# Rotary embedding in three operations ahead of the head norms, queries' norm and transposes beside the key product, first loads on two queues

## The chip, the cores and the metric

The kernel runs on one core of one Trainium2 chip. The metric is the device time of one execution in microseconds (us), as the median of several executions. Engines are called PE (TensorE matmul, with PEld for its weight loads), DVE (VectorE), ACT (ScalarE), POOL (GpSimd) and SP (SyncE, which here only issues DMAs). Each engine works through its own instructions in order; what a program leaves to the scheduler is only the order in which they stand there.

## The reference

The reference is a network in two parts over a sequence of 256 tokens with 1024 features, all in float32. The change touches only the first part's projections and the latent attention ("b") that follows them:

```python
def apply_rope(x, positions):               # r = 32
    ang = positions[..., None] * inv_freq
    cos = jnp.cos(ang)[:, :, None, :]; sin = jnp.sin(ang)[:, :, None, :]
    x1, x2 = xf[..., : r // 2], xf[..., r // 2:]
    out = jnp.concatenate([x1 * cos - x2 * sin, x2 * cos + x1 * sin], axis=-1)
...
xn = rms_norm(h, norm_mix_g)
proj = jnp.einsum('bsd,de->bse', xn, w_in)
qa, ka, va, c_q, c_kv, k_rope = jnp.split(proj, cuts, axis=-1)
qa = rms_norm(qa.reshape(b, s, 8, 64), qnorm_a_g)
ka = rms_norm(ka.reshape(b, s, 8, 64), knorm_a_g)
...
qb = jnp.einsum('bsr,re->bse', rms_norm(c_q, cq_norm_g), w_uq).reshape(b, s, 8, 96)
kv = jnp.einsum('bsr,re->bse', rms_norm(c_kv, ckv_norm_g), w_ukv)
k_nope, vb = kv[..., :64], kv[..., 64:]
kb = jnp.concatenate([k_nope, broadcast(k_rope)], axis=-1)
qb = rms_norm(qb, qnorm_b_g); kb = rms_norm(kb, knorm_b_g)
qb = jnp.concatenate([qb[..., :64], apply_rope(qb[..., 64:], positions)], axis=-1)
kb = jnp.concatenate([kb[..., :64], apply_rope(kb[..., 64:], positions)], axis=-1)
out_b = causal_block_attention(qb, kb, vb)
```

Behind it come the output product, a feed-forward network, and the second part (two layers with attention, 32 experts and a gated embedding). The rotation turns pairs of a head's features with the same angle, so it leaves the head's sum of squares as it is; a head's norm factor is the same before and after it.

## The kernel before

Tokens lie on the partitions in two tiles t of 128. Weights stream from HBM through an arena of 21 buffers in panels that SP issues in program order (L299). A float32 product is made of three matmuls: `split` (L528 to 538) takes a weight block and writes a rounded copy hi and the remainder lo into one of five `s` buffers. The copy is made by ACT (L536), every sixth by POOL (L534); the subtraction by DVE (L537), every fifth by POOL (L537). `mm3` (L540 to 543) then issues x_hi·hi (L541), x_hi·lo (L542) and x_lo·hi (L543), per k block of 128 features and per t: six matmuls for a k block. `steps_of` splits two blocks ahead.

PE and SP execute in the order of the code. ACT, DVE and POOL get their order from a scheduler that goes by its own estimates. What follows a product (copies out of PSUM, squares for the norms) is put into the list `late` and issued by `flush` after the first two splits of the next product.

The order of the first part: transposes of x (`xt_feats`, L501, evicted by ACT L518 and DVE L519), product cq in two halves (the other transposes of x go on beside the first), the tables of the rotation (L1278 to 1307), ckv, qa, uq (two halves of 384 columns, evicted by `uq_done`, L1373), ukv (evicted by `ukv_done`, L1403), ka (`kproj`, L1411), va (`vproj`, L1440), transposes of the normed queries and keys of attention b (`heads_T`, L1454 and L1455: PE L730, ACT L731), then the attention stream (L1491), into which the rest of va is woven. `Rstd` (L481 to 496) squares x on ACT (L488), four operations, and makes the row factor r. `head_ss` squares on ACT (L603) and sums on DVE (L604). `rsqrt` (L456 to 479) is a chain of DVE operations; one call, 32 values wide, serves queries and keys (L1418 to 1420). After it POOL multiplies the queries by their factor (L1424, two instructions), DVE rotates queries and keys (`rope`, L752 to 762: six operations for the queries' t and six for the keys' t), DVE and POOL norm the keys (L1428, L1430). All this is written between the first k block of ka and the rest of it.

At the start, SP issues the identity, two tiles of x, the first weight panel, two more tiles of x and further panels; ACT issues `small`, the table of gains (L382 to 404).

## Time and profile before

| | |
|---|---|
| median of 3 runs | 880.39 us (879.73 to 885.22) |
| the profiled execution | 883.1 us, span in the trace 881.3 us |
| mean granted PE clock | 0.971 |
| PE busy | 829.3 us (94%) |
| DVE busy | 512.2 us (58%) |
| ACT busy | 453.0 us (51%) |
| POOL busy | 225.0 us (26%) |
| DMA | 200.05 MB, mean 227 GB/s |

The median is the kernel's time. The span is what the trace covers; 1.8 us of the profiled execution lie around it. Busy shares are means over stages with different limits, so what matters is which wait of PE ends last in a stage. [...] Matmul rows that follow one another closely are pipelined, so the distance from start to start is what one costs, not its own length.

### The profile page before, as it was taken

To read this page: it belongs to the slowest core of one execution; us is meant where nothing else is said; L and a number is where in the kernel's file an instruction comes from. 1 tells how busy PE (TensorE), PEld (TensorE's weight loads), DVE (VectorE), ACT (ScalarE), POOL (GpSimd) and SP (SyncE) were. 2 spreads that over 40 slices of the span, in tenths; PEclk is the share of its full clock that TensorE was granted. 3 is DMA by queue.
4 is the path that set the end of the run, shared out by engine and by line. 5 is a ranking of instruction groups with operands and counts; after the bars stand their busy time and mean duration, and the time that the engine had idled before them with its cause. 6 is when DMAs were issued, how large, how long until landed. Compare 5 with 4: busy or idle time off the path is not lost. (4 is left out here: it accounts for less than half of the span.)

```text
span 881.3 us, 15729 instructions
## 1 busy us (share of the span) xinstructions
PE 829.3 (94%) x5660; PEld 647.4 (73%) x5660; DVE 512.2 (58%) x1479; ACT 453.0 (51%) x1106; POOL 225.0 (26%) x293
## 2 busy tenths in 40 slices
PE   8997999999999999999899999965899899999997
PEld 5995878999999988686667666635587778666656
DVE  5669656755454567678664544321688765543355
ACT  6675875544444456267675133420666774232463
POOL 2225542322222234214453200000122355000011
PEclk9998999999999999999799999995999899999999
DMA  9990429655556542446015699999463515799961
GB/s 307 385 375 31 146 81 399 237 191 171 198 179 188 182 144 96 161 141 237 1 50 197 254 378 406 408 397 379 157 207 129 208 66 193 293 384 406 408 262 49
DMA packets 85137, 200.05 MB, mean 227 GB/s; under 512 B 5776, under 2 KB 27584, under 8 KB 85056
## 3 DMA queue, kind: packets, MB, share of 16 engines
q1 hardware_dynamic: 82704, 195.61, 61.1%
q10 hardware_dynamic: 2352, 3.40, 1.1%
q8 instruction: 46, 0.75, 0.3%
q14 instruction: 35, 0.29, 0.1%
HBM read 197.93 MB, written 1.06 MB: 226 GB/s over the span
## 5 line engine op out<-in xcount | busy, mean ns | idle before, releaser
L537 DVE TENSOR_TENSOR s<-a,s 128x512 fp32r<-128x512 f32 (+3 forms) x281 | 189.5, 685 | 121.7 <-ACT s L536 87.0
L536 ACT CAST s<-a 128x512 fp32r<-128x512 f32 (+3 forms) x294 | 172.6, 600 | 169.8 <-PE pj L543 71.7
L541 PE MATMUL pj<-s,a 128*128 128x512 f32 (+3 forms) x456 | 176.1, 386 | 4.6 <-ACT a L518 3.0
L542 PE MATMUL pj<-s,a 128*128 128x512 f32 (+3 forms) x456 | 170.5, 374 | 5.9 <-DVE s L537 5.8
L543 PE MATMUL pj<-s,a 128*128 128x512 f32 (+3 forms) x456 | 170.4, 374 | 1.3 <-DVE a L519 1.2
L537 POOL TENSOR_TENSOR s<-a,s 128x512 fp32r<-128x512 f32 (+3 forms) x71 | 90.1, 1269 | 304.6 <-ACT s L536 246.6
L541 PEld LDWEIGHTS pj<-s,a 128*128 128x128 f32 x456 | 86.4, 190 | 24.1 <-issue 5.6
L534 POOL TENSOR_SCALAR s<-a 128x512 fp32r<-128x512 f32 (+3 forms) x58 | 40.3, 696 | 242.3 <-PE pj L543 113.9
L542 PEld LDWEIGHTS pj<-s,a 128*128 128x128 f32 x456 | 86.7, 190 | 20.1 <-DVE s L537 7.8
L543 PEld LDWEIGHTS pj<-s,a 128*128 128x128 f32 x456 | 86.6, 190 | 18.2 <-DVE a L519 3.6
L1517 PE MATMUL f<-a,s 128*128 128x256 f32 x256 | 72.6, 284 | 0.0
L1519 PE MATMUL f<-a,s 128*128 128x256 f32 x256 | 72.4, 283 | 0.0
L1518 PE MATMUL f<-a,s 128*128 128x256 f32 x256 | 72.4, 283 | 0.0
L1027 PE MATMUL gu<-a,xe 128*32 128x256 f32 x1024 | 58.7, 380 | 0.7 <-DVE xe L1002 0.7
L1027 PEld LDWEIGHTS gu<-a,xe 128*32 128x32 f32 x1024 | 32.5, 110 | 28.4 <-issue 4.9
L541 PE MATMUL acc<-s,a 128*128 128x512 f32 x128 | 50.1, 391 | 0.0
L542 PE MATMUL acc<-s,a 128*128 128x512 f32 x128 | 49.9, 390 | 0.0
L543 PE MATMUL acc<-s,a 128*128 128x512 f32 x128 | 49.8, 389 | 0.0
L1518 PEld LDWEIGHTS f<-a,s 128*128 128x128 f32 x256 | 49.1, 192 | 0.2
L1517 PEld LDWEIGHTS f<-a,s 128*128 128x128 f32 x256 | 49.1, 192 | 0.2
L1519 PEld LDWEIGHTS f<-a,s 128*128 128x128 f32 x256 | 49.1, 192 | 0.0
L638 POOL TENSOR_SCALAR P<-P,nd 128x128 f32<-128x128 f32 x64 | 30.2, 483 | 58.7 <-DVE nd L633 18.1
(365 smaller groups left out, 1426.1 us busy)
## 6 DMA issues: line engine op xcount, KB each, us to landing
a<-in_w_ff_dram SPq DMA_DIRECT2D x32, 1024.0 KB, 5.5
a<-in_moe_w_gate_dram SPq DMA_DIRECT2D x64, 512.0 KB, 6.8
a<-in_moe_w_up_dram SPq DMA_DIRECT2D x64, 512.0 KB, 7.5
a<-in_moe_w_down_dram SPq DMA_DIRECT2D x32, 1024.0 KB, 8.8
a<-in_a_w_in_dram SPq DMA_DIRECT2D x10, 1024.0 KB, 5.1
a<-in_ple_w_gate_dram SPq DMA_DIRECT2D x8, 1024.0 KB, 15.6
a<-in_w_in_dram SPq DMA_DIRECT2D x6, 1024.0 KB, 14.4
a<-in_w_o_dram SPq DMA_DIRECT2D x4, 1024.0 KB, 13.8
```

The lines of the kernel that those rows point to most:

```text
L534: G.tensor_scalar(hi, wv, 1.0, 0.0, OP.mult, OP.add)
L536: A.copy(hi, wv)
L537: (G if nsplit[0] % 5 == 2 else V).tensor_tensor(lo, wv, hi.bitcast(F32), OP.subtract)
L541: mm(ps, xh, hi, start=st, stop=False)
L542: mm(ps, xh, lo, start=False, stop=False)
L543: mm(ps, xl, hi, start=False, stop=sp)
L638: G.tensor_scalar(p[:, o0:o0 + n], p[:, o0:o0 + n], rc[:, t, i:i + 1], 1.0, OP.mult, OP.mult)
L1027: mm(b[32 * e:32 * e + 32, 0:256], T.xe[:, k, 32 * e:32 * e + 32], w, start=k == 0, stop=k == 7)
L1517: mm(o, hi[:, fs], xt[0][:, k], start=st, stop=False)
L1518: mm(o, hi[:, fs], xt[1][:, k], start=False, stop=False)
L1519: mm(o, lo[:, fs], xt[0][:, k], start=False, stop=sp)
```

## The change

Four things are done. The tiles of x for features 0 to 511 are issued by ACT ahead of `small`, and SP issues the first weight panel in their place. The squares of x and the chain for r are written after the first half of cq instead of ahead of the transposes. The rotation's table holds cos and sin (with the sign in it) for both halves, so a rotation is two multiplications and an addition, in place; the keys' rotation is done for both t at once in `ckv_done`, the queries' in `uq_done(1)`, before the norms. `rsqrt` is called apart for queries and keys, 16 wide; the queries' factor, and POOL's multiplication by it, are issued in `uq_done(1)`. The queries' transposes are woven into ka's k blocks on PE; the keys' stay where they were.

```diff
--- before.py
+++ after.py
@@ -386,10 +386,12 @@
     h = take("h", [2, D])
     W = Stream(arena, weights())
     small = const.tile([128, I["c_small"].shape[1]], F32, name="small")
-    nc.scalar.dma_start(small, I["c_small"])
     for c in range(2):
         for t in range(2):
-            nc.sync.dma_start(h[:, t, c * 512:(c + 1) * 512], I["x"][0, t * 128:(t + 1) * 128, c * 512:(c + 1) * 512])
+            (nc.sync if c else nc.scalar).dma_start(h[:, t, c * 512:(c + 1) * 512],
+                                                    I["x"][0, t * 128:(t + 1) * 128, c * 512:(c + 1) * 512])
+        if not c:
+            nc.scalar.dma_start(small, I["c_small"])
         W.room(NB - 1 - 2 * c)
     posi = const.tile([128, 2], I32, name="posi")
     nc.sync.dma_start(posi, I["positions"].rearrange("o (t p) -> p (o t)", p=128))
@@ -749,17 +751,13 @@
                 v = v.rearrange(f"p ({' '.join(names)}) -> p {' '.join(names)}", **dict(zip(names, shape)))
             return v
 
-    def rope(dst1, dst2, x1, x2, w, t, nh, eng):
-        sh = [128, nh, 16]
-        tb = [rt[:, w, i, t].unsqueeze(1).to_broadcast(sh) for i in range(4)]
-        uvzy = sq2("ru")[:, 0:64 * nh].rearrange("p (a h d) -> p a h d", a=4, h=nh)
-        u, v, z, y = [uvzy[:, i] for i in range(4)]
-        eng.tensor_tensor(u, x1, tb[0], OP.mult)
-        eng.tensor_tensor(v, x2, tb[1], OP.mult)
-        eng.tensor_tensor(z, x2, tb[2], OP.mult)
-        eng.tensor_tensor(y, x1, tb[3], OP.mult)
-        eng.tensor_tensor(dst1, u, v, OP.subtract)
-        eng.tensor_tensor(dst2, z, y, OP.add)
+    def rope(dst, x, tb):
+
+        n = x.shape[1]
+        u, v = sq2("ru")[:, 0:64 * n].rearrange("p (w h a d) -> w p h a d", w=2, a=2, d=16)
+        V.tensor_tensor(u, x, tb[0], OP.mult)
+        V.tensor_tensor(v, x[:, :, ::-1], tb[1], OP.mult)
+        V.tensor_tensor(dst, u, v, OP.add)
 
 
     def load_wr(l):
@@ -1253,13 +1251,7 @@
     st = Stage(STAGE)
     xt = new_xt("xt")
     rs = Rstd("r1")
-    for c in range(2):
-        for t in range(2):
-            rs.add(c, t)
     drain(xt_feats(hsrc, 0, 4, [(xt, "mix", 0)]))
-    r = rs.get()
-    r2 = st(2)
-    V.tensor_tensor(r2, r, r, OP.mult)
 
     ssx = st(8)
     cq = take("cq", [2, 768])
@@ -1274,6 +1266,12 @@
 
     drain(proj(xt, "cq", 384, cq_done(0),
                mid=xt_feats(hsrc, 4, 8, [(xt, "mix", 0)])))
+    for c in range(2):
+        for t in range(2):
+            rs.add(c, t)
+    r = rs.get()
+    r2 = st(2)
+    V.tensor_tensor(r2, r, r, OP.mult)
 
     pf = tiny.tile([128, 2], F32, tag="pf", name="pf")
     V.tensor_copy(pf, posi)
@@ -1296,15 +1294,15 @@
     V.tensor_scalar(kk, kk, -1.0, math.pi / 2, OP.mult, OP.add)
     A.activation(sn, ang, AF.Sin)
     A.activation(cs, kk, AF.Sin)
-    rt = st(2, 4, 2, 16)
+    rt = st(2, 2, 2, 2, 16)
     for w in range(2):
         ro, _n = _SMALL_COLS[("ropeq", "ropek")[w]]
         g1 = small[:, ro:ro + 16].unsqueeze(1).to_broadcast([128, 2, 16])
         g2 = small[:, ro + 16:ro + 32].unsqueeze(1).to_broadcast([128, 2, 16])
-        V.tensor_tensor(rt[:, w, 0], cs, g1, OP.mult)
-        V.tensor_tensor(rt[:, w, 1], sn, g2, OP.mult)
-        V.tensor_tensor(rt[:, w, 2], cs, g2, OP.mult)
-        V.tensor_tensor(rt[:, w, 3], sn, g1, OP.mult)
+        V.tensor_tensor(rt[:, w, 0, :, 0], cs, g1, OP.mult)
+        V.tensor_tensor(rt[:, w, 0, :, 1], cs, g2, OP.mult)
+        V.scalar_tensor_tensor(rt[:, w, 1, :, 0], sn, -1.0, g2, OP.mult, OP.mult)
+        V.tensor_tensor(rt[:, w, 1, :, 1], sn, g1, OP.mult)
 
 
     vps = bank("vps")
@@ -1331,6 +1329,8 @@
             A.activation(junk[:, :256], ps[t][:, 0:256], AF.Square, accum_out=ssx[:, 4 + t:5 + t])
             A.activation(junk[:, 256:288], ps[t][:, 256:288], AF.Square, scale=r[:, t:t + 1],
                          accum_out=sskr[:, t:t + 1])
+        kv = kr.rearrange("p t (a d) -> p t a d", a=2)
+        rope(kv, kv, [rt[:, 1, i] for i in range(2)])
 
     drain(proj(xt, "ckv", 288, ckv_done))
     qk = take("qk", [2, 2, 512])
@@ -1370,6 +1370,12 @@
 
     qbr = take("qbr", [2, 8, 96])
     ssq = st(2, 2, 8)
+    rsb = st(2, 2, 8)
+
+    def rsqrt_b(i):
+        xb = tiny.tile([128, 32], F32, tag="xb", name="xb", bufs=1)[:, 0:16]
+        V.tensor_scalar(xb, ssq[:, i].rearrange("p t h -> p (t h)"), 1.0 / 96, EPS, OP.mult, OP.add)
+        rsqrt(rsb[:, i].rearrange("p t h -> p (t h)"), xb, 16)
 
     def uq_done(c):
         def f(ps):
@@ -1377,6 +1383,13 @@
                 pv_ = ps[t].rearrange("p (h d) -> p h d", d=96)
                 A.activation(qbr[:, t, 4 * c:4 * c + 4], pv_, AF.Copy, scale=rqk[:, t:t + 1])
                 head_ss(ssq[:, 0, t, 4 * c:4 * c + 4], pv_, 4, 96, rqk[:, t:t + 1])
+            if c:
+                for t in range(2):
+                    qv = qbr[:, t, :, 64:96].rearrange("p h (a d) -> p h a d", a=2)
+                    rope(qv, qv, [rt[:, 0, i, t].unsqueeze(1).to_broadcast([128, 8, 2, 16]) for i in range(2)])
+                rsqrt_b(0)
+                for t in range(2):
+                    G.tensor_tensor(qbr[:, t], qbr[:, t], rsb[:, 0, t].unsqueeze(2).to_broadcast([128, 8, 96]), OP.mult)
         return f
 
     for c in range(2):
@@ -1414,27 +1427,21 @@
 
     for t in range(2):
         V.tensor_scalar(ssq[:, 1, t], ssq[:, 1, t], sskr[:, t:t + 1], None, OP.add)
-    xb = tiny.tile([128, 32], F32, tag="xb", name="xb", bufs=1)
-    V.tensor_scalar(xb, ssq.rearrange("p a t h -> p (a t h)"), 1.0 / 96, EPS, OP.mult, OP.add)
-    rsb = st(2, 2, 8)
-    rsqrt(rsb.rearrange("p a t h -> p (a t h)"), xb, 32)
+    rsqrt_b(1)
     kbr = take("kbr", [2, 8, 96])
-    krr = st(2, 32)
     for t in range(2):
-        G.tensor_tensor(qbr[:, t], qbr[:, t], rsb[:, 0, t].unsqueeze(2).to_broadcast([128, 8, 96]), OP.mult)
-        rope(qbr[:, t, :, 64:80], qbr[:, t, :, 80:96], qbr[:, t, :, 64:80], qbr[:, t, :, 80:96], 0, t, 8, V)
-        rope(krr[:, t, 0:16].unsqueeze(1), krr[:, t, 16:32].unsqueeze(1),
-             kr[:, t, 0:16].unsqueeze(1), kr[:, t, 16:32].unsqueeze(1), 1, t, 1, V)
         V.tensor_tensor(kbr[:, t, :, 0:64], kvb[:, t, :, 0:64],
                         rsb[:, 1, t].unsqueeze(2).to_broadcast([128, 8, 64]), OP.mult)
-        G.tensor_tensor(kbr[:, t, :, 64:96], krr[:, t].unsqueeze(1).to_broadcast([128, 8, 32]),
+        G.tensor_tensor(kbr[:, t, :, 64:96], kr[:, t].unsqueeze(1).to_broadcast([128, 8, 32]),
                         rsb[:, 1, t].unsqueeze(2).to_broadcast([128, 8, 32]), OP.mult)
     caus = take("caus", [256])
     V.tensor_scalar(caus, C("ndm"), -1e33, NEG, OP.is_lt, OP.mult)
     dil = take("dil", [8, 256])
     v0 = vd[:, :]
     nc.scalar.dma_start(dil, bass.AP(tensor=v0.tensor, offset=v0.offset, ap=[[1, 128], [384, 8], [1, 256]]))
-    drain(kproj)
+    qTb = take("qTb", [8, S])
+    weave(kproj, heads_T(qTb, lambda t, f: qbr[:, t, f], 8, 96, qsc[:96, 1:2]), 0.7, -1.0)
+    drop("qbr")
 
 
     vproj = proj(xt, "va", 512, qkv_done(2))
@@ -1449,11 +1456,9 @@
             (V if t else G).tensor_tensor(qv, qv, rsa[:, c, t].unsqueeze(2).to_broadcast([128, 8, 64]), OP.mult)
     for _ in range(2):
         next(vproj)
-    qTb = take("qTb", [8, S])
     kTb = take("kTb", [8, S])
-    drain(heads_T(qTb, lambda t, f: qbr[:, t, f], 8, 96, qsc[:96, 1:2]))
     drain(heads_T(kTb, lambda t, f: kbr[:, t, f], 8, 96, gain("kb", 0, 96)))
-    drop("qbr", "kbr")
+    drop("kbr")
     qTa = take("qTa", [4, S])
     kTa = take("kTa", [4, S])
     mixT = new_xt("mixT")
```

POOL, around the key product, before. `s` are the split buffers, a_262 is the panel of ukv, a_282 and a_361 are the two panels of ka, a_399 and a_446 those of va, a_641 the queries, a_877 the keys:

```order
L537 TENSOR_TENSOR s<-a_262,s 128x512
L534 TENSOR_SCALAR s<-a_262 128x512
L534 TENSOR_SCALAR s<-a_361 128x512
L537 TENSOR_TENSOR s<-a_282,s 128x512
L537 TENSOR_TENSOR s<-a_399,s 128x512
L1424 TENSOR_TENSOR a_641<-a_641,stage 128x768 x2
L534 TENSOR_SCALAR s<-a_399 128x512
L1430 TENSOR_TENSOR a_877<-stage 128x8x32 x2
```

And of the change (line numbers are two higher for the same code; a_236 is ukv, a_256 and a_361 are ka, a_399 is va, a_645 the queries, a_906 the keys):

```order
L539 TENSOR_TENSOR s<-a_236,s 128x512
L536 TENSOR_SCALAR s<-a_236 128x512
L1392 TENSOR_TENSOR a_645<-a_645,stage 128x768 x2
L536 TENSOR_SCALAR s<-a_361 128x512
L539 TENSOR_TENSOR s<-a_256,s 128x512
L539 TENSOR_TENSOR s<-a_399,s 128x512
L1435 TENSOR_TENSOR a_906<-stage 128x8x32 x2
L536 TENSOR_SCALAR s<-a_399 128x512
```

The queries' multiplication has moved from behind all of ka's splits to ahead of them: ahead of the copy of ka's block 5 (first panel row a_361) and the subtraction of ka's block 3 (a_282 before, a_256 now).

DVE, from the last subtractions of ukv on, before:

```order
L537 TENSOR_TENSOR s<-a_262,s 128x512 x3
L604 TENSOR_REDUCE stage<-sq 128x4 x2
L537 TENSOR_TENSOR s<-a_282,s 128x512 x2
L604 TENSOR_REDUCE stage<-sq 128x4 x3
L1416 TENSOR_SCALAR stage<-stage 128x8
L604 TENSOR_REDUCE stage<-sq 128x4
L1416 TENSOR_SCALAR stage<-stage 128x8
L537 TENSOR_TENSOR s<-a_282,s 128x512
```

And of the change, from the same place:

```order
L539 TENSOR_TENSOR s<-a_236,s 128x512 x3
L606 TENSOR_REDUCE stage<-sq 128x4
L758 TENSOR_TENSOR ru<-a_645,stage 128x256
L759 TENSOR_TENSOR ru<-a_645,stage 128x256
L606 TENSOR_REDUCE stage<-sq 128x4
L760 TENSOR_TENSOR a_645<-ru 128x8x32
L758 TENSOR_TENSOR ru<-a_645,stage 128x256
L759 TENSOR_TENSOR ru<-a_645,stage 128x256
L1377 TENSOR_SCALAR xb<-stage 128x16
L539 TENSOR_TENSOR s<-a_256,s 128x512
L760 TENSOR_TENSOR a_645<-ru 128x8x32
L470 TENSOR_SCALAR rs<-xb 128x16
```

The queries' rotation and the start of their factor now stand between ukv's subtractions and ka's. Between the subtractions of ka's block 1 and block 2 stand then the rest of that chain (nine operations), four sums and the two additions that were L1416 and are L1429.

ACT, at the start, before (a_109 is the second panel of cq, a_99 is x, a_142 its transpose):

```order
L536 CAST s<-a_109 128x384
L488 ACTIVATE junk,ss<-a_99 128x512 x4
L518 ACTIVATE a_142<-tps,small 128x256 x2
L536 CAST s<-a_109 128x384
L518 ACTIVATE a_142<-tps,small 128x256
L536 CAST s<-a_109 128x384
```

And of the change:

```order
L538 CAST s<-a_109 128x384
L490 ACTIVATE junk,ss<-a_99 128x512
L520 ACTIVATE a_142<-tps,small 128x256
L490 ACTIVATE junk,ss<-a_99 128x512 x2
L520 ACTIVATE a_142<-tps,small 128x256 x2
L490 ACTIVATE junk,ss<-a_99 128x512
L538 CAST s<-a_109 128x384
L520 ACTIVATE a_142<-tps,small 128x256
```

The four squares have not left this place: the scheduler puts them between the same evictions, now one after one square instead of after four.

## Rows read from the trace of the kernel before

**Rows 1.** Waits of PE, 0 to 140 us; us in total, times, longest.
```profile
PE pj L542 <- DVE s L537: 5.4, 2, 5.0
PE pj L541 <- ACT a L518: 1.3, 1, 1.3
...
PE pj L543 <- DVE a L519: 0.8, 2, 0.6
```

**Rows 2.** Timeline of PE: start, length, instruction, xcount, idle before and releaser.
```profile
69.65 0.39 PE L541 MATMUL pj<-s,a 128*128 128x512 f32 x1
70.41 0.50 PE L542 MATMUL pj<-s,a 128*128 128x512 f32 x1 [0.37 <-DVE s L537]
...
79.88 0.39 PE L541 MATMUL pj<-s,a 128*128 128x512 f32 x1
85.28 0.80 PE L542 MATMUL pj<-s,a 128*128 128x512 f32 x1 [5.01 <-DVE s L537]
...
89.87 3.66 PE L730 MATMUL htp<-ident_r,a 128*96 128x128 f32 x32
```

**Rows 3.** Windows: busy time of each engine in each stretch.
```profile
core 0: us, PE busy (x) PEld busy (x) DVE busy (x) ACT busy (x) POOL busy (x), PEclk, DMA share, GB/s
4.00:5.00 1.00, 1.00 (x6) 0.47 (x5) 0.00 (x0) 0.00 (x0) 0.00 (x0) 1.00 0.56 142
...
80.00:85.30 5.30, 0.29 (x3) 0.02 (x1) 5.30 (x26) 1.71 (x3) 2.10 (x3) 0.76 0.00 0
85.30:88.00 2.70, 2.70 (x6) 2.13 (x7) 2.70 (x5) 0.18 (x1) 2.30 (x2) 0.50 0.00 0
```

**Rows 4.** Timeline of DVE, 61 to 94 us.
```profile
62.22 0.69 DVE L537 TENSOR_TENSOR s<-a,s 128x512 fp32r<-128x512 f32 x1 [2.35 <-POOL s L534]
62.83 1.01 DVE L604 TENSOR_REDUCE stage<-sq 128x4 f32<-128x384 f32 x2
...
68.51 0.67 DVE L1416 TENSOR_SCALAR stage<-stage 128x8 f32<-128x8 f32 x1
...
69.67 0.69 DVE L537 TENSOR_TENSOR s<-a,s 128x512 fp32r<-128x512 f32 x1
70.27 1.27 DVE L1418 TENSOR_SCALAR xb<-stage 128x32 f32<-128x32 f32 x1
...
81.14 0.28 DVE L759 TENSOR_TENSOR ru<-a,stage 128x128 f32<-128x128 f32 x1
81.35 0.28 DVE L760 TENSOR_TENSOR ru<-a,stage 128x128 f32<-128x128 f32 x1
...
84.54 0.68 DVE L537 TENSOR_TENSOR s<-a,s 128x512 fp32r<-128x512 f32 x1
...
91.37 0.18 DVE L465 TENSOR_TENSOR rs<-rs 128x32 f32<-128x32 f32 x1
...
92.72 0.19 DVE L479 SCALAR_TENSOR_TENSOR stage<-rs 128x32 f32<-128x32 f32 x1
```

**Rows 5.** Timeline of POOL, 55 to 94 us.
```profile
68.53 0.62 POOL L534 TENSOR_SCALAR s<-a 128x512 fp32r<-128x512 f32 x1 [6.35 <-DMA a<-vd]
70.13 1.37 POOL L537 TENSOR_TENSOR s<-a,s 128x512 fp32r<-128x512 f32 x1 [0.97 <-POOL s L534]
...
76.60 3.86 POOL L1424 TENSOR_TENSOR a<-a,stage 128x768 f32<-128x768 f32 x2 [0.81 <-DVE stage L479]
```

**Rows 6.** Timeline of all engines, 0 to 20 us.
```profile
1.18 0.89 SPq L392 DMA_DIRECT2D a<-in_x_dram  x2
...
2.12 0.43 SPq L299 DMA_DIRECT2D a<-in_w_in_dram  x1
...
8.66 0.44 PE L541 MATMUL pj<-s,a 128*128 128x384 f32 x1 [1.25 <-ACT a L518]
...
11.75 0.63 ACT L488 ACTIVATE junk<-a 128x512 f32<-128x512 f32 x1
...
17.49 0.44 PE L543 MATMUL pj<-s,a 128*128 128x384 f32 x1 [0.64 <-DVE a L519]
```

## The prediction

> **What bounds the kernel now.** The page says that PE is busy 94% of the span, so a change elsewhere pays only where PE waits. I therefore read the waits of PE first, for 0 to 140 us, the stretch in which the diff moves anything; behind the attention the order of all engines is the same but for some rows of DVE. [rows 1] Few waits are left there: 5.4 us for DVE's lo of a split (two waits, one of them 5.0), 1.3 for ACT's copy of a transpose and 0.8 for DVE's. The first is in the key and value products, the others are at the head.
>
> I then looked at PE's timeline around the long wait. [rows 2] From 70.41 to 79.88 stand 41 matmuls, so one costs 9.47 / 41 = 0.23 us. In ka's block 2 the L541 of 69.65 is followed by an L542 at 70.41 instead of 69.88: 0.5 late. In va's block 1 the L541 of 79.88 is followed by an L542 at 85.28 instead of 80.11: 5.2 late. From there 11 matmuls take 85.28 to 89.87 = 4.59 us; at 0.23 they would take 2.5, so another 2.1 go. [...] So this stage loses 0.5 + 5.2 + 2.1 = 7.8 us, and that is what the change can win here.
>
> DVE's timeline says what it is late with: [rows 4] va's subtraction starts at 84.54, right after 24 rope operations on the same engine, which are done from 79.05 to 84.54. Nothing is slow about the subtraction itself, it is queued.
>
> **What the change removes and adds.** The rope operations leave that place, so the 5.2 and the 2.1 go, unless something takes their place. I follow the new DVE queue from the end of ukv's subtractions, 62.83 (the start of what follows the last one of 62.22). [rows 4]
> - Two sums, 1.01 for both, started 0.95 apart from what follows.
> - Six rope operations of 128x256. The trace has 128x128, whose starts lie 0.20 apart (81.14, 81.35), and 128x512 in the subtraction, 0.61 (62.22 to 62.83). Between them 128x256 is 0.20 + 0.41 / 3 = 0.34; six make 2.0. The bounds are 0.20 (1.2) and 0.61 (3.7).
> - Three small operations at about 0.1 (0.3) and ka's first two subtractions, 0.61 each (1.2). That is 67.3; ka's block 0 and 1 need theirs at 67.1 and 68.5 (69.65 less 11 and less 5 matmuls), and block 0's stands one place earlier, at about 66.2. Both are in time.
> - The rest of the queries' chain: before, eight dependent operations from 91.37 to 92.72 with the last one's 0.19 make 1.54; one more is 0.17. So the queries' factor is ready at T0 = 69.0.
>
> Now POOL starts the queries' multiplication: 3.86 us for two [rows 5], to 72.95. Behind it in POOL's queue stand two pieces of the key product, as the order shows: the copy of ka's block 5 (0.62, before at 68.53), then the subtraction of ka's block 3 (1.37, before at 70.13). That subtraction now ends at 69.0 + 0.1 + 3.86 + 0.62 + 1.3 = 74.9, and PE's L542 of block 3 is due at 69.88 + 6 x 0.23 = 71.3. So PE waits 3.6 us there even if nothing else is late. This is the first price of the change.
>
> The second is on DVE. It has four sums and two additions of 128x8 ahead of the subtraction of ka's block 2. Such an addition took 0.67 at 68.51 with POOL's copy beside it (68.53, 0.62), and the 1.27 of L1418 at 70.27 end at 71.54 with POOL's subtraction (70.13 to 71.50) [rows 4, 5]: DVE stood still until POOL's instruction ended. Beside 1.93-us instructions of POOL the same gives: sums to 70.1, first addition to 71.0, second to 72.95, the subtraction after POOL's copy at 73.6, done at 74.2. So the L542 of ka's block 2 starts at 74.25 instead of 69.88, 4.4 late, and block 3's at 75.6 finds its lo ready. I take 4.4; the lower bound is the 3.6 above, the upper one comes with the rope operations at 0.61: T0 is 1.7 later, so 6.1.
>
> [...]
>
> A wait of 4.4 us is nearly as long as the 5.0 that halved the clock. I take the same clock loss, 2.1, with bounds 0 (the clock holds) and 3.1 (it stays low half as long again). So the stage loses 6.5 after and 7.8 before: 1.3 us won.
>
> **The other parts.** The queries' 16 transposes move from after the value blocks into ka. All 32 take 3.66 us on PE [rows 2] and each costs the same anywhere, so 0; the queries are ready at 72.95, and the first transposes stand behind ka's block 3, which ends after 76. If that cover went, PE would wait for POOL there instead of at block 3, no more. The keys' rotation is now three DVE operations of 128x64 at under 0.20 each [rows 4] beside the qa product, whose subtractions have 1 to 2 us in hand: 0; without that cover 0.5. The rotation's table has eight operations as before: 0. Queries' and keys' `rsqrt` apart add nine small operations, about 1.5 us of DVE, which hold back the later subtractions of ka; these follow PE's own delay: 0, and 1.5 without that cover.
>
> At the head, SP spent 0.89 us on two tiles of x before the first panel (issued at 2.12) [rows 6]; now ACT issues these tiles and the panel goes 0.9 earlier. The first matmul, at 8.66, waited 1.25 for ACT, which had begun when the panel landed. Not all of the 0.9 arrives, since the tiles and the panel share the transfers; in 4 to 5 us the DMA share was 0.56 [rows 3], so there was a gap of 0.4 us to fill. The squares (0.63 each [rows 6]) hold up the copies out of PSUM: the waits of the second set, up to the 0.64 at 17.49. In the new order one copy stands after one square, but all four are still ahead of a copy of cq's block 6, so most of that wait moves there. I take 1.0 for the head; the bounds are 0 and the 2.1 of all its waits [rows 1].
>
> [...]
>
> **Sum.** 1.3 + 1.0 = 2.3. The profiled execution took 883.1, of which 1.8 lie around the span of 881.3; it becomes 880.8. It is 2.7 above the median, which becomes 880.4 - 2.3 = 878.1.
>
> **The rivals.**
> - The clock holds through the new wait (0.2). It is shorter than the one before, and on both sides of it PE works without gaps. Against it: 5.0 us sufficed before, and the new one is only 0.6 shorter. The 2.1 are won too: 876.0.
> - Slower than before (0.15): the new wait is longer than the old. Place: the subtraction of ka's block 2 and the queue ahead of it. If the rope operations cost 0.61 each, the wait is 6.1, and with 3.1 for the clock the stage loses 9.2 instead of 7.8; with a head that wins nothing, 881.8. It decides when that subtraction ends later than 69.88 + 5.7 = 75.6 (5.7 + 2.1 is the 7.8 of before), with the head's 1.0 later than 76.6. For it: the operand is in strided pieces of 16, which no row of before has in this size. Against it: 128x128 in the same strides was at 0.20.
> - The key product does not wait (0.07). POOL's two splits would have to be ready in time, which needs the queries' factor before about 65.5; by the queue above it is not there before 68. The whole 7.8 and the head's 1.0 are won: 871.6.
> - The two queues do nothing (0.03): the transfers share the same engines and the first panel lands when it did. Then 1.0 less is won: 879.1.
>
> **How the numbers follow.** The forecast has 0.55, with a range of its own from 876.5 (wait 3.6, head 1.8) to 879.7 (wait 5.4, head 0.4). The rivals have 0.2, 0.15, 0.07 and 0.03. The range from 874.0 to 882.0 takes in the forecast, the held clock with its own 2 us, the slower case and the two queues; it leaves out the case without a wait and the tails of the others. A measurement can tell about 1%, 8.8 us. To win that much, the whole 7.8 and over 1.0 at the head would be needed: 0.04. To lose it, the new wait would have to be some 11 us longer than forecast, which no row bears out: 0.02. Within 1%: 0.94.
>
> **What would show it.** Right: in the trace after, no long wait at va's block 1; an L542 of ka's block 2 (or 3) some 4 us late, released by DVE or by POOL's subtraction; POOL's two 128x768 instructions at about 69 to 73, with DVE's additions beside them stretched to over 1 us; a granted clock of 0.50 after it; the first panel's matmul at about 8.0. Wrong: rope operations at over 0.4 us; POOL's multiplication starting before 67 or after 71; a wait at va's block 0 or 1 as before, now behind the keys' norm; or waits at the head that are all still there.

## The result, and the profile after

The changed kernel takes 876.09 us in the median of 6 runs (872.97 to 876.67), the kernel before 881.51 in 6 runs beside it (879.73 to 885.22). The ratio is 0.9929 with a 95% interval of 0.9903 to 0.9955. The profiled execution took 875.73, its span is 873.9; PE is busy 824.7 us (94%), the mean granted clock, the share of PE's full clock that the chip granted, is 0.979 (0.971 before). So the change gains 5.4 us, 0.6%; the forecast was 2.3 us (878.1), with a range of 874.0 to 882.0. A later comparison, with 5 runs of the changed kernel and 17 of the one before, gave 875.84 and 880.13: 4.3 us.

Line numbers of the changed kernel are two higher in the helpers: L543, L544, L545 are the three matmuls of `mm3`, L539 the subtraction, L536 POOL's copy. The waits of PE in its trace, 0 to 140 us (us in total, times, longest), answer to [rows 1]:

```profile
PE pj L544 <- DVE s L539: 3.8, 3, 2.5
PE warm L378 <- DVE xc L1739: 1.1, 1, 1.1
PE pj L543 <- ACT a L520: 0.8, 1, 0.8
PE tps L503 <- DMA a<-in_x_dram: 0.8, 1, 0.8
PE ops L656 <- ACT PT L650: 0.2, 1, 0.2
```

The 5.0 us in the value product are gone. In their place stands one wait of 2.5 for DVE's subtraction (the other 1.3 us of that first line are two waits at the head, 0.2 and 1.1), and the waits for the head's copies, 1.3 and 0.8 before, have become one of 0.8. PE's timeline (start, length, instruction, idle before and its releaser), around the new wait, against [rows 2]:

```profile
69.19 0.39 PE L543 MATMUL pj<-s,a 128*128 128x512 f32 x1
72.10 0.53 PE L544 MATMUL pj<-s,a 128*128 128x512 f32 x1 [2.52 <-DVE s L539]
...
76.08 0.40 PE L545 MATMUL pj<-s,a 128*128 128x512 f32 x1
```

It is in ka's block 2, the place that the forecast named. The L544 was due at 69.19 + 0.23 = 69.42 and is 2.7 late. The 10 matmuls from 72.10 to 76.08 take 3.98 us, where 0.23 each would be 2.3. The windows of the same stretch, against [rows 3]:

```profile
core 0: us, PE busy (x) PEld busy (x) DVE busy (x) ACT busy (x) POOL busy (x), PEclk, DMA share, GB/s
69.40:72.10 2.70, 0.18 (x1) 0.00 (x0) 2.67 (x5) 1.17 (x3) 2.70 (x3) 1.00 0.00 0
72.10:76.30 4.20, 4.20 (x11) 3.25 (x12) 4.17 (x10) 0.62 (x1) 1.67 (x2) 0.59 0.01 2
76.30:85.00 8.70, 8.70 (x47) 7.20 (x46) 6.91 (x13) 6.00 (x10) 4.27 (x4) 1.00 0.00 0
```

The granted clock falls after this wait too (0.59 over 72.10 to 76.30), and is back by 76.3. DVE and POOL beside it, against [rows 4] and [rows 5]; first DVE's timeline:

```profile
62.84 0.41 DVE L758 TENSOR_TENSOR ru<-a,stage 128x256 f32<-128x256 f32 x1
63.17 0.42 DVE L759 TENSOR_TENSOR ru<-a,stage 128x256 f32<-128x256 f32 x1
...
68.20 0.18 DVE L481 SCALAR_TENSOR_TENSOR stage<-rs 128x16 f32<-128x16 f32 x1
...
69.40 0.63 DVE L1429 TENSOR_SCALAR stage<-stage 128x8 f32<-128x8 f32 x1
...
70.38 1.07 DVE L1429 TENSOR_SCALAR stage<-stage 128x8 f32<-128x8 f32 x1
71.37 0.68 DVE L539 TENSOR_TENSOR s<-a,s 128x512 fp32r<-128x512 f32 x1
```

and POOL's:

```profile
68.53 2.90 POOL L1392 TENSOR_TENSOR a<-a,stage 128x768 f32<-128x768 f32 x2 [6.80 <-ACT sq L605]
71.39 1.13 POOL L536 TENSOR_SCALAR s<-a 128x512 fp32r<-128x512 f32 x1
72.49 1.27 POOL L539 TENSOR_TENSOR s<-a,s 128x512 fp32r<-128x512 f32 x1
```

A rotation operation of 128x256 starts 0.33 after the one before it, as interpolated. The queries' factor is written at 68.20, POOL's multiplications run from 68.53 to 71.4, and the two additions of 128x8 are stretched to 0.63 and 1.07 beside them. The second ends with POOL's pair, and the subtraction that PE waits for comes right behind. (The profile names a square of ACT as what released POOL's pair, because it ended just before, at 68.51. By the program the pair waits for the rotated queries and for their factor, not for that square.)

How far each kernel is ahead can be read where PE starts the same instruction: the first transposes of cq, the first score matmul of the attention, and the first matmul of the output product. This table is from the timelines of all kernels below:

| kernel | cq's transposes | first scores | output product |
|---|---|---|---|
| before | 40.08 | 93.66 | 119.22 |
| changed | 39.74 | 89.52 | 115.72 |
| changed, profiled again | 39.92 | 88.42 | 114.62 |
| head_only | 40.06 | 93.26 | 118.80 |
| rope3_only | 40.57 | 91.93 | 117.49 |
| qT_late | 39.99 | 89.69 | 115.26 |
| rope_early | 39.95 | 86.86 | 115.15 |
| tables_late | 38.41 | 88.19 | 114.39 |
| qkn_pool | 39.85 | 86.76 | 116.09 |
| ms_qkn | 40.34 | 87.23 | 115.14 |
| best2 | 38.51 | 85.40 | 114.74 |
| best3 | 38.80 | 85.70 | 113.61 |

The change is 0.3 us ahead at 40, 4.1 at the attention's start and 3.5 at the output product. From there the two first traces keep 3.5 us for the next 300 us. At the end they are 7.4 apart, because a stretch of low clock at 427.5 to 437.7 (granted clock 0.50) stands in the trace before and not in the one after. Behind it, at 440, the change is 8.1 ahead. The last experiment bears on whether this stretch is part of what the change does.

### The profile page after: what moved, and what is told of

The parts are those of the page before. It is cut to its first block, busy times and chain, and to the rows that moved or that the text cites. A ratio compares the mean times of both kernels' runs of the same rounds, so it can differ in the third digit from the quotient of the medians.

```text
span 873.9 us, 15726 instructions
## 1 busy us (share of the span) xinstructions
PE 824.7 (94%) x5660; PEld 644.6 (74%) x5660; DVE 512.8 (59%) x1476; ACT 452.6 (52%) x1106; POOL 223.9 (26%) x293
## 3 DMA queue, kind: packets, MB, share of 16 engines
HBM read 197.93 MB, written 1.06 MB: 228 GB/s over the span
## 5 line engine op out<-in xcount | busy, mean ns | idle before, releaser
L539 DVE TENSOR_TENSOR s<-a,s 128x512 fp32r<-128x512 f32 (+3 forms) x281 | 189.7, 686 | 115.7 <-ACT s L538 81.2
L543 PE MATMUL pj<-s,a 128*128 128x512 f32 (+3 forms) x456 | 176.4, 387 | 4.2 <-ACT a L520 2.6
L544 PE MATMUL pj<-s,a 128*128 128x512 f32 (+3 forms) x456 | 170.5, 374 | 4.2 <-DVE s L539 4.2
L545 PE MATMUL pj<-s,a 128*128 128x512 f32 (+3 forms) x456 | 170.3, 373 | 0.5 <-DVE a L521 0.4
L539 POOL TENSOR_TENSOR s<-a,s 128x512 fp32r<-128x512 f32 (+3 forms) x71 | 89.2, 1257 | 310.5 <-ACT s L538 261.0
L543 PEld LDWEIGHTS pj<-s,a 128*128 128x128 f32 x456 | 86.4, 190 | 23.1 <-issue 6.2
L536 POOL TENSOR_SCALAR s<-a 128x512 fp32r<-128x512 f32 (+3 forms) x58 | 40.5, 699 | 233.8 <-PE pj L545 109.8
L544 PEld LDWEIGHTS pj<-s,a 128*128 128x128 f32 x456 | 86.6, 190 | 18.6 <-DVE s L539 6.5
L545 PEld LDWEIGHTS pj<-s,a 128*128 128x128 f32 x456 | 86.3, 189 | 16.8 <-DVE a L521 2.1
L543 PE MATMUL acc<-s,a 128*128 128x512 f32 x128 | 50.1, 391 | 0.0
L544 PE MATMUL acc<-s,a 128*128 128x512 f32 x128 | 49.9, 390 | 0.0
L545 PE MATMUL acc<-s,a 128*128 128x512 f32 x128 | 49.8, 389 | 0.0
L640 POOL TENSOR_SCALAR P<-P,nd 128x128 f32<-128x128 f32 x64 | 29.7, 476 | 54.5 <-DVE nd L635 18.8
```

Of the source, the lines that this page charges most:

```text
L536: G.tensor_scalar(hi, wv, 1.0, 0.0, OP.mult, OP.add)
L539: (G if nsplit[0] % 5 == 2 else V).tensor_tensor(lo, wv, hi.bitcast(F32), OP.subtract)
L543: mm(ps, xh, hi, start=st, stop=False)
L544: mm(ps, xh, lo, start=False, stop=False)
L545: mm(ps, xl, hi, start=False, stop=sp)
L640: G.tensor_scalar(p[:, o0:o0 + n], p[:, o0:o0 + n], rc[:, t, i:i + 1], 1.0, OP.mult, OP.mult)
```

## Experiments

Each kernel was timed beside the kernel before. The traces say what happened in the first 119 us; the medians also hold the stretches of low clock behind them.

**The head alone.** The kernel before with the edits to the first loads and the squares, as in the diff of the change, and nothing else.

> The kernel before with only the head's edits: first loads on two queues, squares of x after cq's first half. In the changed kernel PE was 2.3 us ahead at 17 us and only 0.34 ahead at 25 us, after a wait of 1.05 us for DVE's subtraction at 23.1. Theory 1: the lead is lost because DVE's rotation tables wait for ACT's sine with its table load at about 20 us, whatever the order of the table's own operations; then this kernel too is 2 us ahead at 17 us and 0.3 to 0.5 ahead at 40 us, and its median is 0.3 to 0.5 under that of before. Rival: it is lost because the changed table's operations stand in another order ahead of a subtraction; then 1.7 or more are kept here, median 1.7 to 2.3 under before. The wait of 5 us in the value product stays by both.

Measured: 879.84 (12 runs) against 880.53, ratio 0.9993 (0.9975 to 1.0012). PE's waits in its trace, 15 to 26 us:

```profile
20.03 0.45 PE L544 MATMUL pj<-s,a 128*128 128x384 f32 x1 [0.24 <-DVE s L539]
23.44 0.44 PE L544 MATMUL pj<-s,a 128*128 128x384 f32 x1 [1.04 <-DVE s L539]
```

PE is 2.0 us ahead at 17 us and 0.02 ahead at 40: the old table, in its old order, loses the lead in the same place. Against the expectation not even 0.3 is kept, so the head's edits alone are worth nothing that shows. (Its first product starts at 8.28, where the changed kernel with the same first loads has 7.98; a difference of 0.3 here is one between executions.) The rival of the table's order falls.

**The tables after cq's second half.** In the changed kernel, the DVE operations and ACT's sines of the rotation's tables are written behind the second half:

```diff
-    pf = tiny.tile([128, 2], F32, tag="pf", name="pf")
-    ...
     vps = bank("vps")
     ...
     drain(proj(xt, "cq", 384, cq_done(1)))
+    pf = tiny.tile([128, 2], F32, tag="pf", name="pf")
+    ...
```

> The changed kernel with the rotation's tables (DVE operations and ACT's two sines) written after cq's second half instead of ahead of it. Theory: the head's lead of 2 us is lost at 20 to 23 us because a subtraction of cq's second half stands on DVE behind table operations that wait for ACT's sine; here 1.3 to 2 us of lead are left at 40 us, and the median is 1 to 2 under the changed kernel. Rival 1: the lead is lost anyway, to the weights' transfers or to the addition for logc that waits for PE; then no faster. Rival 2: the sine's table load (1.28 us on ACT) now holds up a copy for the second half and costs as much as was won.

Measured: 875.89 (12 runs), ratio 0.9948 (0.9927 to 0.9968). The wait of 1.05 at 23 us is gone and only 0.34 at 19.7 is left; the lead is 1.7 at 40 us and 4.8 at the output product, 1.3 more than in the changed kernel's first profile, in which the clock fell behind ka's wait as it does here. So this is where the head's gain went: DVE's table operations wait for ACT's sine and its table load (1.28 us on ACT, from 19.89 in the changed kernel), and a subtraction of the second half stands behind them. In the changed kernel these are DVE's first operation behind the sine and that subtraction, and PE's matmul that waits for it:

```profile
21.45 0.19 DVE L1304 SCALAR_TENSOR_TENSOR stage<-rope,small 128x32 f32<-128x32 f32 x1 [1.08 <-ACT rope L1295]
...
22.52 0.54 DVE L539 TENSOR_TENSOR s<-a,s 128x384 fp32r<-128x384 f32 x1
...
23.11 0.45 PE L544 MATMUL pj<-s,a 128*128 128x384 f32 x1 [1.05 <-DVE s L539]
```

The second part of the expectation, a lower median, did not come. Its trace has a stretch of low clock at 422 to 433 again, and such stretches differ between executions by more than 1.3, so the median neither shows the 1.3 nor speaks against it.

**The rotation alone.** The kernel before with the new `rope` and its table, so with the rotation in three operations, at its old place:

```diff
-        rope(qbr[:, t, :, 64:80], qbr[:, t, :, 80:96], ..., 0, t, 8, V)
-        rope(krr[:, t, 0:16].unsqueeze(1), ..., 1, t, 1, V)
+        qv = qbr[:, t, :, 64:96].rearrange("p h (a d) -> p h a d", a=2)
+        rope(qv, qv, [rt[:, 0, i, t].unsqueeze(1).to_broadcast([128, 8, 2, 16]) for i in range(2)])
+        if not t:
+            ...
+            rope(krr..., kv, [rt[:, 1, i] for i in range(2)])
```

> The kernel before with only the rotation in three operations, at its old place after the norms (keys for both tiles at once), queries' norm and transposes where they were. Theory: the wait in the value product's second block is the rotation's time on DVE; 24 operations become 9, at 0.33 each for 256 columns (changed kernel's trace) and about 0.15 for 64, of which 8 stand ahead of the subtraction: about 2.2 us instead of 5.5, so the wait falls from 5.2 to 2 to 2.5 and the clock's loss from 2.1 to 1.7: 3 us under before. Rival: DVE stands there because POOL's multiplication holds it up, so that fewer operations do not shorten it: wait over 4, median as before.

Measured: 879.3 (12 runs), ratio 0.9983 (0.9961 to 1.0004). The wait in the value product is 3.3, between theory and rival. Its DVE timeline says why:

```profile
79.53 1.69 DVE L756 TENSOR_TENSOR ru<-a,stage 128x256 f32<-128x256 f32 x1
81.14 0.82 DVE L757 TENSOR_TENSOR ru<-a,stage 128x256 f32<-128x256 f32 x1
...
82.49 0.41 DVE L756 TENSOR_TENSOR ru<-a,stage 128x256 f32<-128x256 f32 x1
```

The first two operations took 1.69 and 0.82 instead of 0.41, while POOL multiplied the queries (3.85 us from 77.08) and copied a block; the rest ran at full pace. So part of the old wait was the number of operations, which the three-operation form cures, and part was DVE held up by POOL, which it does not. In the trace it is 1.7 ahead at the output product, and 0.5 of a slower head (40.57) has to be added; its head ran at half clock from 10.0 to 13.4. The 3 us under before that the theory named did not come: the median is 1.2 under, and its interval reaches just over no change.

**Queries' transposes back to their old place.** `weave(kproj, heads_T(qTb, ...))` becomes `drain(kproj)`, and `heads_T(qTb, ...)` is issued ahead of `heads_T(kTb, ...)`.

> The changed kernel with the queries' transposes back behind the value product's first three blocks. Theory: a transpose costs PE the same anywhere, and no wait is covered by them; within 0.5 us of the changed kernel. Rival: beside the product they hide a wait or shorten the stage's end; then 1 us or more slower than the changed kernel.

Measured: 874.88 (6 runs), ratio 0.9935 (0.9910 to 0.9960). It is level with the changed kernel's first profile, and the clock fell behind ka's wait in both (49.70 us from cq's transposes to the first scores against 49.78, where the changed kernel's second profile, in which the clock held, has 48.50): 89.69 against 89.52 at the first scores, 115.26 against 115.72 at the output product. Moving the transposes is worth nothing that shows.

**The rotation early, the multiplication not.** The changed kernel with one factor chain 32 wide, POOL's multiplication behind it and the transposes late:

```diff
-                rsqrt_b(0)
-                for t in range(2):
-                    G.tensor_tensor(qbr[:, t], qbr[:, t], rsb[:, 0, t]..., OP.mult)
...
-    rsqrt_b(1)
+    rsqrt_b()
     for t in range(2):
+        G.tensor_tensor(qbr[:, t], qbr[:, t], rsb[:, 0, t]..., OP.mult)
         V.tensor_tensor(kbr[:, t, :, 0:64], ...)
```

> The changed kernel with one factor chain, 32 wide, for queries and keys as before, so that POOL's multiplication of the queries comes after the key product's splits again, and the queries' transposes at their old place; the rotation stays early. Theory: the 2.7 us wait at ka's third block is POOL's multiplication, beside which DVE's two small additions stand still; here it is gone. In va's second block a wait of 1 to 2.5 is left, because POOL copies that block behind the multiplications. 1 to 3 us under the changed kernel. Rival: the wait at ka's third block comes from DVE's own queue (rotation, chain, sums) and stays at 1 us or more; then no faster than the changed kernel.

Measured: 874.26 (8 runs), ratio 0.9930 (0.9906 to 0.9954). PE's waits in the key and value products:

```profile
70.15 0.50 PE L544 MATMUL pj<-s,a 128*128 128x512 f32 x1 [0.37 <-DVE s L539]
81.83 0.51 PE L544 MATMUL pj<-s,a 128*128 128x512 f32 x1 [0.22 <-DVE s L539]
```

The 2.7 us are gone although the rotation still stands on DVE where the changed kernel has it, and the clock does not fall (the matmuls behind the wait of 0.37 stay 0.23 apart). So the rotation on DVE is not what makes the new wait. The run alone does not show that POOL's multiplication is, because it also takes the queries' chain out of DVE's queue ahead of that subtraction. The rows of the changed kernel divide the two. Its two additions of 128x8 held DVE for 0.54 and 0.99 us up to the next start, where one beside an idle POOL held it for 0.14 (69.53 to 69.67 in the kernel before): 1.25 of the 2.7 us are DVE held up by POOL, and the rest is the chain and the sums. But DVE alone in time would have won little. In the second profile of the changed kernel POOL's subtraction, behind the pair and the copy, ends at 73.95, and the matmul of ka's block 3 that needs it starts at 74.00, where it was due at 69.36 + 7 x 0.23 = 70.97:

```profile
72.66 1.29 POOL L539 TENSOR_TENSOR s<-a,s 128x512 fp32r<-128x512 f32 x1
...
74.00 0.51 PE L544 MATMUL pj<-s,a 128*128 128x512 f32 x1
```

So DVE's additions and POOL's own split both lead to POOL's multiplication ahead of the key product's splits; the chain on DVE has a share in the first. The expectation's other part did not come: in va's second block 0.22 is left, not 1 to 2.5. Nor do the medians tell this kernel from the changed one (0.9930 against 0.9929 and 0.9950).

The first scores come 6.8 us earlier than before. Of that 4.1 are left at the output product; the rest is lost in the attention's start, which took 28.3 us from first scores to output product instead of 25.6. DVE's timeline there:

```profile
89.29 0.19 DVE L481 SCALAR_TENSOR_TENSOR stage<-rs 128x32 f32<-128x32 f32 x1
89.52 2.14 DVE L1452 TENSOR_TENSOR a<-a,stage 128x512 f32<-128x512 f32 x2
92.65 0.17 DVE L1706 MEMSET stage<- 128x128 f32 x1 [1.00 <-POOL a L1452]
92.73 0.23 DVE L631 CUSTOM_DVE_ANT_0 P<-sps,a 128x128 f32<-128x128 f32 x1
```

The first softmax operation (L631) stands behind attention a's multiplications (L1452) and behind a memset for the second part of the network, which the scheduler puts here and which waits 1.0 for POOL.

**Attention a's multiplications all on POOL.** On the kernel of rope_early, `(V if t else G).tensor_tensor(qv, ...)` becomes `G.tensor_tensor(qv, ...)`.

> The kernel of rope_early with the four multiplications of attention a's queries and keys all on POOL, instead of two on POOL and two on DVE (5.8 us on POOL, none on DVE). In rope_early PE reaches the attention 6.8 us earlier than before and keeps 4.1 of it; theory: the first softmax on DVE stands behind these two multiplications and behind a memset that waits for POOL's, so DVE starts at 92.7 what it could start at 90 to 91; here 1 to 2.6 us more are kept at 118 us, and the median is 1 to 2 under rope_early. Rival: the first softmax is bound elsewhere (ACT's exponentials, POOL's scalings, which now stand behind 5.8 us on POOL); then no faster, or slower by up to 1.

Measured: 875.96 (12 runs), ratio 0.9948 (0.9931 to 0.9964). The rival held: 116.09 at the output product, 0.9 later than rope_early. DVE's timeline shows another reason than the one expected:

```profile
93.59 0.17 DVE L1706 MEMSET stage<- 128x128 f32 x1 [4.22 <-POOL a L1452]
93.67 0.23 DVE L631 CUSTOM_DVE_ANT_0 P<-sps,a 128x128 f32<-128x128 f32 x1
```

Now the memset alone holds the softmax for 4.2 us: it takes over the buffer from which POOL's multiplications read their factors, so it has to wait for the last of them.

**The memset on POOL as well.** `V.memset(kcT, 0.0)` becomes `G.memset(kcT, 0.0)` on top of that.

> The kernel of qkn_pool with one memset of the second part's table (128x128) given to POOL instead of DVE. There it stood ahead of the first softmax on DVE and waited 4.2 us for POOL's multiplications, whose factors lie in a buffer that it takes over. Theory: that wait is what holds up the attention's start; the first softmax starts at 89.5 instead of 93.7, and 2 to 3.5 us more are kept at 118 us (5.5 to 6.8 under before). Rival: POOL's scalings of the softmax, behind the multiplications, become the bound; then less than 1 us more is kept.

Measured: 874.55 (5 runs), ratio 0.9928 (0.9911 to 0.9946).

```profile
89.79 0.28 DVE L631 CUSTOM_DVE_ANT_0 P<-sps,a 128x128 f32<-128x128 f32 x1
```

The softmax starts at 89.79, as the theory had it. At the output product 115.14 instead of 116.09, and 0.5 of a slower head has to be added: 1.4 more are kept, not 2 to 3.5. POOL's timeline, and then DVE's, show the next bound:

```profile
89.95 4.05 POOL L1452 TENSOR_TENSOR a<-a,stage 128x512 f32<-128x512 f32 x4 [5.47 <-DVE stage L481]
...
94.83 1.79 POOL L640 TENSOR_SCALAR P<-P,nd 128x128 f32<-128x128 f32 x2
```

```profile
94.89 1.39 DVE L539 TENSOR_TENSOR s<-a,s 128x512 fp32r<-128x512 f32 x2 [2.59 <-POOL s L536]
96.20 0.28 DVE L631 CUSTOM_DVE_ANT_0 P<-sps,a 128x128 f32<-128x128 f32 x1
```

The scalings of the softmax (L640) stand on POOL behind the four multiplications, and so does the copy of a weight block (L536, at 94.23), for which DVE stands 2.59 us ahead of the next softmax. That one starts at 96.20, in rope_early at 96.19, in qkn_pool at 97.14, and the output product follows 18.95 us behind it in all three; behind the first scalings it follows by 20.0 in the other two and by 20.3 here. So the copy fits better as the bound than the scalings, though no run moves either of them. Both theories had a part of it: first the memset, then POOL.

**Both edits together.** First the tables late and the multiplications on POOL (best2), then the memset on POOL too (best3).

> The two edits above together, on rope_early: rotation early, one factor chain, queries' transposes late, tables after cq's second half, attention a's multiplications all on POOL. If both theories hold, 7 to 8.5 us under the kernel before by 118 us in the trace and in the median; if the attention's start is bound elsewhere, 4 as rope_early.

Measured: 874.33 (6 runs), ratio 0.9936 (0.9911 to 0.9961). 4.5 ahead at the output product: the tables' 1.4 are kept, the attention's start is bound as in qkn_pool.

> The kernel before it with the rotation's tables after cq's second half as well (worth 1.3 us at 118 us in tables_late). 7 to 8 us under before at 118 us if both theories hold, and a median of 872 to 874; with stretches of low clock falling differently, up to 877.

Measured: 873.10 (12 runs) against 880.13, ratio 0.9934 (0.9914 to 0.9953). 5.6 ahead at the output product, less than the 7 to 8 expected: the wait of 2.59 us for POOL's copy is the same as in ms_qkn, at 93.35. In the trace it is 1.0 to 2.1 ahead of the changed kernel and its median is the lowest of all. The interval overlaps with that of the changed kernel beside it (0.9950, 0.9933 to 0.9966), and several other kernels here have a ratio as low, so that it beats the changed kernel is what the traces show up to the output product, and the medians only suggest.

**The changed kernel again.**

> The changed kernel itself, beside the next two on one chip. Theory: of the 7.4 us between the two first profiles 3.5 belong to the change (they stand in the trace by 118 us and stay) and about 4.6 to stretches of low granted clock behind the attention that fall differently in each execution; then the profile here is 3.5 ahead of the first one of before at 118 us again, the low stretches lie elsewhere, and the medians differ by 3.5 to 5. Rival: the change moves the later low stretches away for good; then none at about 420 us here either, and the medians differ by 6 or more.

Measured: 875.84 (5 runs) against 880.13 (17 runs), ratio 0.9950 (0.9933 to 0.9966). Its wait in ka's block 2 is the same 2.52 us, but this time the clock held (1.00 over 72.30 to 76.30). PE's timeline:

```profile
69.36 0.39 PE L543 MATMUL pj<-s,a 128*128 128x512 f32 x1
72.26 0.50 PE L544 MATMUL pj<-s,a 128*128 128x512 f32 x1 [2.52 <-DVE s L539]
72.60 0.39 PE L545 MATMUL pj<-s,a 128*128 128x512 f32 x1
72.83 0.40 PE L543 MATMUL pj<-s,a 128*128 128x512 f32 x1
```

It is 4.6 ahead at the output product, 1.1 more than the first profile of the changed kernel and than the theory had. In the second part of the network the stretch of low clock is back, and not elsewhere, as the theory had it, but at the place where the kernel before has it. Three windows of 11 us from the same place in the program, at the transposes of the second attention, in the first trace before, the first after, and this one:

```profile
423.00:434.00 11.00, 8.59 (x48) 7.15 (x50) 6.15 (x23) 4.92 (x19) 4.29 (x7) 0.70 0.00 1
```

```profile
419.50:430.50 11.00, 8.62 (x78) 6.57 (x80) 8.34 (x35) 7.16 (x26) 6.04 (x11) 1.00 0.01 2
```

```profile
418.50:429.50 11.00, 8.74 (x48) 7.31 (x50) 6.03 (x23) 4.90 (x18) 4.13 (x7) 0.69 0.01 1
```

PE waits 0.72 and 1.82 us there in all three, for the same operations; in the trace before these rows are

```profile
423.59 0.30 PE L730 MATMUL htp<-ident_r,a 128*128 128x128 f32 x1 [0.72 <-DVE a L1571]
425.72 0.55 PE L730 MATMUL htp<-ident_r,a 128*128 128x128 f32 x3 [1.82 <-POOL a L1571]
```

The granted clock (third number from the end of a window) is 0.70, 1.00 and 0.69, and 78 matmuls pass in one case and 48 in the others. So the change does not move this stretch away, as the rival had it. Over the twelve traces of this document the longer wait is always there (1.82 or 1.83 us), and half clock behind it lasts 10.2 us in six (before, after_again, tables_late, qkn_pool, ms_qkn, best2), 3.4 in three (head_only, rope3_only, qT_late) and is absent in three (changed, rope_early, best3): the kernel before stands in the first group beside kernels with the change, and the changed kernel's own two traces stand in two groups. For the kernel before there is one trace only, so how often it has the stretch is not known. The 4.6 us that it costs (the lead goes from 3.5 at 427 to 8.1 at 440) were the larger part of the 7.4 between the first two profiles.

## Why the prediction was right, point by point

**What bounds the kernel.** Right. The long wait was in the stage named, and that is where the gain of the first part comes from.

**The removed wait.** Right. With the rotation gone from the place ahead of va's subtraction no wait is left at va's block 1. rope3_only adds what the prediction did not see: part of those 5.2 us was DVE held up beside POOL's multiplication, and not only the number of operations. The rows of before show it too, just ahead of those of the forecast:

```profile
76.56 2.57 DVE L1428 TENSOR_TENSOR a<-a,stage 128x512 f32<-128x512 f32 x2
79.05 1.55 DVE L757 TENSOR_TENSOR ru<-a,stage 128x128 f32<-128x128 f32 x1
```

The first operation of the rotation took 1.55 us beside POOL's pair (76.60 to 80.46), where the same form took 0.28 later. Of the 24 operations that the forecast counts ahead of the subtraction it was 23; the last stands behind it.

**The new wait.** Right in its place (ka's block 2, released by DVE's subtraction), its cause (POOL's multiplication ahead of the splits, which rope_early and the rows above bear out, on both ways that the forecast named: DVE's additions held up beside it, and POOL's own splits queued behind it) and the clock behind it. Its size was 2.7 us, against 4.4 forecast and a lower bound of 3.6. The mis-sized term is POOL's pair of 128x768, taken at 3.86 from [rows 5]. It took 2.90: in the kernel before, and in rope_early (1.98 and 1.92), it ran beside DVE instructions that read two operands (the keys' multiplications first, then the rotation or subtractions), in the changed kernel beside sums and small additions. That is 1.0. The other 0.6 is the order behind it: the forecast let POOL's copy go ahead of DVE's subtraction, but DVE came first at 71.37 and the copy took 1.13 beside it. The start of the pair, 68.5, is the 69.0 of the forecast less the head's 0.45 at that point. The rotation's 0.34 an operation was 0.33.

**The clock.** 2.1 was taken. It was 1.7 in the first profile (3.98 us for 10 matmuls at 2.3), and nothing in the second. The granted clock fell behind the same wait in qT_late and tables_late as well (in tables_late the two matmuls from 71.28 on start 0.43 apart, where 0.23 is the distance at full clock). So the first rival, a clock that holds, is what some executions do; the forecast and this rival are both right in a part of the runs. That the result, 876.1, lies on this rival's 876.0 is luck: in the profile of one of its executions the clock did fall.

**The head.** Wrong as a step, small in the sum. I took 1.0 from PE's waits and asked what each edit does to them, but did not follow DVE's queue to the next place. The first product started 0.7 earlier (7.98), the two waits for DVE's copies went, and PE was 2.3 us ahead at 17 us, more than the 1.0 forecast and than its upper bound of 2.1. (Part of the 0.8 that is left at the first product is a price that the forecast did not name: ACT's first copy out of PSUM, at 7.45, waits 0.55 for `small`, which now stands behind the two tiles of x on ACT's queue.) Then cq's second half waited for a subtraction behind the rotation's tables, and 0.3 was left. head_only keeps nothing, tables_late keeps 1.7: the gain went into a wait for ACT's sine. Taken at 1.0, the head's term measured 0.3 in one profile and 0.2 in the other.

**Transposes, keys' rotation, tables, second chain.** Right at 0 for the transposes, as qT_late is level, and for the table's own operations, as head_only with the old ones has the same wait behind them (1.04 against 1.05). The other two have no run of their own; no wait of PE appears where their cover was named.

**What was left out.** The attention's start, a term that the forecast put at nothing. Where PE comes 4.1 us earlier there, 3.5 are left at the output product, and of 6.8 in rope_early 4.1. The forecast took the gain at the end of the stage as the gain of the kernel; DVE's and POOL's queues at the start of the next stage were not looked at.

**The sum.** 1.3 was forecast for the stage; at the first scores it was 4.1 less the head's 0.3, or 3.8: 3.0 from the waits (0.5 and 5.2 before, 2.7 after), 0.4 from the clock, and 0.4 that I can't place. With the head's 0.3 and the 0.6 lost later the change gains 3.5 us, or 4.6 where the clock holds. The medians say 4.3 and 5.4. What lies between would fit low clock in the second part, which differs between executions; for the median executions, of which there is no trace, this is argued and not shown. The forecast was 878.1, the result is 876.1: inside the range given, and 0.4 below the lower end of the forecast's own range. The errors are larger than this: the stage won 3.8 where 1.3 was forecast, the head 0.3 where it was 1.0, and 0.6 were lost later where nothing was. That the sum comes out near is in part their cancelling, and the range of 8 us is wider than any of them.

## What to carry to other kernels

Work moved off the queue that PE waits for has to be put ahead of something else; what it costs there is read from the other engine's queue, and an operation's time taken from a row next to one kind of neighbour need not hold next to another (3.86 us and 2.90 us for the same pair here). A gain at the end of a stage is a gain of the kernel only if the next stage can start earlier: the same question, who is late next, has to be asked on every engine at the start of the next stage. Where two profiles differ by more than the stage that was changed, compare the starts of the same instructions along the trace before explaining the difference.

## What the runs showed of the hardware

The same wait of PE is followed by half clock in one execution and not in the next. A wait of 2.52 us in ka's block 2 left the clock at 1.00 in one trace and brought it to 0.59 over 4.2 us in another of the same kernel; waits of 0.72 and 1.82 us at the second attention were followed by 10.2 us of half clock in the trace before and in the second of the changed kernel, at a cost of about 4.6 us, and by none in the first of the changed kernel. In half clock that is 0 or 3.4 us behind the wait of 2.52 in two profiles of one kernel (0.59 over 4.2 us lacks as much as 0.50 over 3.4).

In these traces POOL and DVE slowed each other beyond what one would take from their separate busy times: two multiplications of 128x768 on POOL took 2.90 us beside sums and small additions, and 3.85 to 3.90 beside DVE's multiplications and subtractions of two operands. Two of these multiplications took 2.57, against 1.72 in the changed kernel beside POOL's smaller ones (128x256). An addition of 128x8 on DVE took 1.07 beside POOL's multiplication; in the kernel before one took 0.23 while POOL was idle. The sums kept their pace: three took 1.06 together from 68.30 on, almost all of it beside the pair, 0.35 each, against two in 0.73 beside an idle POOL in rope_early.
